# Differential attention heads: the row norm's squares folded in half, high and low part in one product with ones

## The chip, the core and the metric

The kernel runs on one core of one Trainium2 chip. The metric is device time in microseconds of one execution; the time before is the median of three runs. The engines are named as the profile names them: PE (TensorE, matrix products; PEld is its weight load), DVE (VectorE), ACT (ScalarE), POOL (GpSimd) and SP (SyncE, which only issues transfers here). SBUF is the on-chip memory of 128 partitions, PSUM the accumulator memory that PE writes.

## The reference, cut to what matters

One encoder layer of width 1024 over 512 tokens and 16 meta tokens: a stick-breaking attention branch with 8 heads, a differential attention branch with 8 heads, gates, an output projection, and a feed-forward part. All data are float32. The change is in the differential heads, in the norm of each head's output over its 128 channels:

```python
def rmsnorm(x, g):
    xf = x.astype(jnp.float32)
    y = xf * lax.rsqrt(jnp.mean(xf * xf, axis=-1, keepdims=True) + EPS)
    return (y * g.astype(jnp.float32)).astype(x.dtype)
...
    s = jnp.where(mask, s + bias[None, :, None], -jnp.inf)
    p = jax.nn.softmax(s, axis=-1)
    w = p[:, :, 0] - lam * p[:, :, 1]
    return jnp.einsum('bhqk,bhkd->bhqd', w.astype(v.dtype), v)
...
        o_df = (rmsnorm(o_df, subln_g[l]) * (1.0 - lam_init)).transpose(0, 2, 1, 3).reshape(B, L_pad, DF_V_W)
```

## The kernel before, in words

**Products in high and low parts.** Matrix operands are split into a high part (a copy rounded to fp32r, mostly by ACT) and a low part (what the rounding lost, by DVE or POOL); `split` (lines 77 to 81) issues both, at line 78 the high part and at line 81 the low one. A product of two split operands is three PE instructions, lines 296 to 298 in `mm3`: high by high, high by low, low by high.

**The differential stage.** A loop runs over 8 heads. Each head's `df_head` is a generator that yields four to six times; in between, the loop inserts pieces of other work: the next head's projections of q, k and v (`halves`, `kv_units`, `v_units`) and the partial projections of finished pairs of heads (`y_units`, whose results are copied to tiles `y_out` by ACT at line 785 and added into DRAM by transfers that POOL issues at lines 787 and 789). A head computes scores for four blocks of queries (lines 695 and 696 on PE, the biased maximum at line 699 on DVE, the exponentials at line 723 on ACT, the two maps' combination at lines 726 to 729 on DVE), turns the maps (lines 563 and 564), multiplies them with v in `weighted` (lines 296 to 298, 583, 584; the result is a PSUM tile `z`), and then norms its output.

**The norm.** The output stands with its 128 channels on the partitions and 512 tokens along the row, so that the sum over channels is a sum over partitions. It is made on PE: a product with `ones_r`, a 128x128 matrix of 1/128, gives each partition the mean. For heads 0 to 6:

- line 751: ACT copies the output from PSUM to the tile `of` (128x512);
- line 753: POOL squares it into `sq`;
- line 78: ACT casts `sq` into the high part `sqh`, and at line 81 POOL writes the low part `sql`;
- lines 758 and 759: PE multiplies `ones_r` with `sql` and with `sqh` into one PSUM tile `tr`;
- lines 760 to 765: logarithm and exponential on ACT make the reciprocal root, DVE multiplies, ACT and DVE write the normed output's parts `o_h` and `o_l`.

Lines 756 to 765 are the function `norm`, which is not run at once: it is put into the list `late` and taken out in the next head, between the scores of the second and the third block. The tiles `sqh` and `sql` use the buffers of `a_h` and `a_l`, the turned maps, which PE has read by then. Head 7 has no next head: its squares and low part are on DVE, and its norm follows one gate product later.

**What sets the order.** Only the kernel's opening has an order written by hand. In the rest a scheduler orders each engine's instructions by dependencies, by the order of the program and by its own estimate of times, and places semaphore waits. Each engine then runs its instructions strictly in that order. Weights are loaded by SP (line 210) into three buffers, split into `wh` and `wl` two or three pieces ahead of their use, and POOL issues, as background work, transfers (line 151) that prepare sums of later weights in DRAM.

Of the kernel before, what the change touches and what calls it, by code (L numbers as in the profile page):

```python
# [9 lines left out]
F32 = mybir.dt.float32  # L10
F32R = mybir.dt.float32r
BF16 = mybir.dt.bfloat16
AF = mybir.ActivationFunctionType
ALU = mybir.AluOpType
AX = mybir.AxisListType

P = 128
D = 1024
SEQ = 512
# [5 lines left out]
NH = 8  # L25
# [16 lines left out]
def block_kernel(ctx: ExitStack, tc: tile.TileContext, x, meta, norm_mix_g, w_in, w_gate, b_gate,  # L42
                 lam_q1, lam_k1, lam_q2, lam_k2, subln_g, w_br_sb, w_br_df, w_out, norm_ffn_g,
                 w_ffn_gate, w_ffn_up, w_ffn_down, norm_final_g, out):
    nc = tc.nc
# [15 lines left out]
    def tr_tile():  # L61
        return ps_mm.tile([P, 512], F32, tag="mm", name="tr")

    def z_tile():
        return ps_z.tile([P, 2, 512], F32, tag="z", name="z")
# [9 lines left out]
    cast = {}  # L75

    def split(hi, lo, src, lo_eng=None, hi_copy=None, after=None):
        cast["last"] = (hi_copy or nc.scalar.copy)(hi, src)  # L78
        if after:
            behind(cast["last"], after)  # L80
        cast["lo"] = (lo_eng or nc.vector).tensor_tensor(lo, src, hi.bitcast(F32), op=ALU.subtract)  # L81

    def behind(ins, name):
        tc.add_manual_dep(ins.ins, cast[name].ins.name,
                          mybir.DependencyInfo(mybir.DependencyClass.Sync, mybir.DependencyReason.DATA))
# [283 lines left out]
    ones_r = const.tile([P, P], F32R, name="ones_r")  # L369
# [29 lines left out]
    ap_ = att.enter_context(tc.tile_pool(name="att", bufs=1))  # L399
# [285 lines left out]
    def df_head(h, d, o_h, o_l):  # L685
        q, k = d["q"], d["k"]
        bias = ap_.tile([P, L], F32, tag="bias", name="bias")
        nc.gpsimd.tensor_scalar(bias, dist, -(2.0 ** -(h + 1)), None, op0=ALU.mult)
        mx = small.tile([P, NQ, 2], F32, tag="mx", name="mx", bufs=2)
        ls = small.tile([P, NQ, 2], F32, tag="ls", name="ls", bufs=2)  # L690
        prs = [ap_.tile([P, 2, 144 + t * P], F32, tag=f"w{t}", name="pr") for t in range(NQ)]

        def score(o, t, c, k0, k1):
            qs = slice(t * P, (t + 1) * P)
            nc.tensor.matmul(o, lhsT=q[c][:, qs], rhs=k[c][:, 0, k0:k1], start=True, stop=False)  # L695
            nc.tensor.matmul(o, lhsT=q[c][:, qs], rhs=k[c][:, 1, k0:k1], start=False, stop=True)  # L696

        def biased(t, c, zz, po, bb):
            nc.vector.tensor_tensor_reduce(po, zz, bb, scale=1.0, scalar=-3.0e38, op0=ALU.add, op1=ALU.max,  # L699
                                           accum_out=mx[:, t, c:c + 1])  # L700

        def scores(t):
            n = 144 + t * P
            z = z_tile()
            for c in range(2):
                score(z[:, c, 0:max(n, 256)], t, c, 0, max(n, 256))
            for c in range(2):
                biased(t, c, z[:, c, 0:n], prs[t][:, c], bias[:, L - n:L])
            maps(t)

        def scores3(c):
            two = lambda v: v.rearrange("p (a b) -> p a b", a=2)
            z = z_tile()
            for hf in range(2):
                score(z[:, hf, 0:HL], 3, c, hf * HL, (hf + 1) * HL)
            biased(3, c, z[:, :, 0:HL], two(prs[3][:, c]), two(bias))

        def maps(t):
            pr = prs[t]
            nm = small.tile([P, 2], F32, tag="nm", name="nm")  # L720
            nc.vector.tensor_scalar(nm, mx[:, t], -1.0, None, op0=ALU.mult)
            for c in range(2):
                nc.scalar.activation(pr[:, c], pr[:, c], AF.Exp, bias=nm[:, c:c + 1], accum_out=ls[:, t, c:c + 1])
            with tc.high_priority(offset=EVAC):
                rc = small.tile([P, 2], F32, tag="rc", name="rc")
                nc.vector.reciprocal(rc, ls[:, t])
                nc.vector.tensor_tensor(rc, rc, cn, op=ALU.mult)
                nc.vector.tensor_scalar(pr[:, 0], pr[:, 0], rc[:, 0:1], None, op0=ALU.mult)
                nc.vector.scalar_tensor_tensor(pr[:, 0], pr[:, 1], rc[:, 1:2], pr[:, 0], op0=ALU.mult, op1=ALU.add)

        scores(0)
        scores(1)
        yield 1
        if late:
            late.pop(0)()
        scores(2)
        yield 1
        scores3(0)
        yield 1
        scores3(1)  # L740
        maps(3)
        turned, av = attn_out(lambda t, k0, k1: prs[t][:, 0, k0:k1], d, 64)
        yield 3 if h < NH - 1 else 2
        turned()
        yield 2
        ps = av()
        of = ap_.tile([P, SEQ], F32, tag="of", name="of")
        sq = ap_.tile([P, SEQ], F32, tag="sq", name="sq")
        sqh = ap_.tile([P, SEQ], F32R, tag="a_h", name="sqh")
        sql = ap_.tile([P, SEQ], F32R, tag="a_l", name="sql")  # L750
        nc.scalar.copy(of, ps)
        eng = nc.gpsimd if h < NH - 1 else nc.vector
        eng.tensor_tensor(sq, of, of, op=ALU.mult)
        split(sqh, sql, sq, lo_eng=eng)

        def norm():
            pv = tr_tile()
            nc.tensor.matmul(pv, lhsT=ones_r, rhs=sql, start=True, stop=False)
            nc.tensor.matmul(pv, lhsT=ones_r, rhs=sqh, start=False, stop=True)
            nc.scalar.activation(sq, pv, AF.Ln, bias=eps_c)  # L760
            cast["norm"] = nc.scalar.activation(sq, sq, AF.Exp, scale=-0.5)
            nc.vector.scalar_tensor_tensor(sq, pv, var_max, sq, op0=ALU.is_le, op1=ALU.mult)
            nc.vector.tensor_tensor(of, of, sq, op=ALU.mult)
            nc.scalar.activation(o_h, of, AF.Copy, scale=g_sub)
            nc.vector.scalar_tensor_tensor(o_l, of, g_sub, o_h.bitcast(F32), op0=ALU.mult, op1=ALU.subtract)

        late.append(norm)


# [138 lines left out]
    def split_part(n, a, b, hi=nc.scalar.copy, lo=nc.gpsimd.tensor_tensor):  # L908
# [25 lines left out]
                            op=ALU.mult)  # L934
# [60 lines left out]
    todo = []  # L995
    for br in range(2):
        name, head = (("y_sb", sb_head), ("y_df", df_head))[br]
        if br:
            nc.gpsimd.memset(a_s, 0.0)
# [150 lines left out]
    def turned(tp_):  # L1150
        cs = slice(tp_ * 256, (tp_ + 1) * 256)
        banks = [z_tile() for _ in range(2)]
        for k in range(0, KT, 2):
            pt = banks[k // 2 % 2][:, k // 4]
            for i in range(2):
                for t in range(2):
                    nc.tensor.transpose(pt[:, (2 * i + t) * P:(2 * i + t + 1) * P],
                                        hn[:, 2 * tp_ + t, (k + i) * P:(k + i + 1) * P], ident)
            for i in range(2):
                g = g_ffn[:, k + i:k + i + 1]  # L1160
                p = pt[:, i * 256:(i + 1) * 256]
                nc.scalar.activation(hT_h[:, k + i, cs], p, AF.Copy, scale=g)  # L1162
                nc.vector.scalar_tensor_tensor(hT_l[:, k + i, cs], p, g, hT_h[:, k + i, cs].bitcast(F32),
                                               op0=ALU.mult, op1=ALU.subtract)
        for k in range(KT):
            p = banks[k // 2 % 2][:, k // 4, k % 2 * 256:(k % 2 + 1) * 256]
            if tp_ == 0:
                nc.scalar.activation(bf[k // 4][0][:, k % 4], p, AF.Copy, scale=g_ffn[:, k:k + 1])
            else:
                x, y = (bf[0][0], bf[0][1]) if k < 4 else (bf[0][1], bf[1][1])  # L1170
                cast["bf"] = nc.vector.scalar_tensor_tensor(y[:, k % 4], p, g_ffn[:, k:k + 1], x[:, k % 4], op0=ALU.mult, op1=ALU.subtract)
# [376 lines left out]
```

## Time and profile before

| | |
|---|---|
| median of 3 runs | 931.77 us (931.14 to 932.34) |
| profiled execution, its own time | 931.87 us |
| span in that profile | 930.1 us |
| instructions | 16033 |
| time of one differential head (281 to 459 us of the span) | 29.6 us |
| granted PE clock, mean | 0.999 |

In rows of the profile a line number such as L758 is a line of the kernel; an arrow reads from right to left, output from inputs; "x7" counts instructions. In rows of the timeline the first number is the start in microseconds from the start of the span, the second the duration, and a bracket tells how long the engine was idle just before and which instruction ended the wait. In the table by stretches each engine has its busy time and its number of instructions, and the last three columns are the granted PE clock (1.00 is full speed), the mean busy share of the 16 DMA engines, and what they moved. Names end without buffer numbers: `sq` of line 1441 and `sq` of line 753 are different tiles.

### The profile page before, as it was taken

Reading aid. Unit: us, or ns where it says so; the run is one execution under the profiler, and the core shown is the slowest. Engines: PE = TensorE matmul, PEld = TensorE weight load, DVE = VectorE, ACT = ScalarE, POOL = GpSimd, SP = SyncE. Lnnn points to the kernel's source line nnn. Section 1 sums busy time; section 2 is a strip of 40 time slices with the busy share of each in tenths; the row PEclk is TensorE's granted clock in tenths of the full one; section 3 lists DMA queues with packets and bytes.
Section 4 is the critical chain, followed back from the end, with each engine's and each line's share of the span. In section 5 each row is a group of like instructions: output and inputs, shape, how many; then the busy total and the mean of one; then the engine's idle time right before and its main releaser. Section 6 shows DMA issues by size and latency. Waiting matters only on the chain.

```text
span 930.1 us, 16033 instructions
## 1 busy us (share of the span) xinstructions
PE 918.8 (99%) x6010; PEld 836.9 (90%) x6010; DVE 734.3 (79%) x1413; ACT 586.1 (63%) x1104; POOL 168.4 (18%) x199
## 2 busy tenths in 40 slices
PE   8999999999999999999999999999999999999997
PEld 5999999998999899998988888899999999988886
DVE  7988877776687767976663787899888888799975
ACT  6765676676666666666665555776555555576554
POOL 3000121222333343344512000001100000000013
PEclk9999999999999999999999999999999999999999
DMA  8525598778777878799987774437744343276542
GB/s 253 139 68 168 143 212 201 169 167 250 191 192 177 217 170 182 181 211 186 197 209 181 215 260 159 127 80 183 169 118 131 91 129 98 88 274 193 192 149 91
DMA packets 155823, 158.41 MB, mean 170 GB/s; under 512 B 6465, under 2 KB 117218, under 8 KB 155746
## 3 DMA queue, kind: packets, MB, share of 16 engines
q1 hardware_dynamic: 132690, 101.61, 36.2%
q0 software_dynamic: 22896, 55.72, 29.2%
q8 instruction: 47, 0.77, 0.3%
q14 instruction: 30, 0.25, 0.1%
q10 hardware_dynamic: 160, 0.07, 0.0%
HBM read 133.64 MB, written 50.86 MB: 198 GB/s over the span
## 4 chain that ended last, share of the span: by engine, by line
PE 94%; DVE 3%; ACT 2%; issue 1%; ACTq 0%; DVEq 0%
PE mm L297 22%; PE mm L296 22%; PE mm L298 22%; PE z L297 7%; PE z L296 7%; PE z L298 7%; PE z L563 2%; PE z L696 1%; PE z L695 1%; PE tr L537 1%; DVE wl L81 1%; DVE hres L1205 1%; PE z L584 1%; PE mm L858 0%; ACT wh L78 0%
## 5 line engine op out<-in xcount | busy, mean ns | idle before, releaser
L296 PE MATMUL mm<-xT_h,wh 128*128 128x264 f32 (+2 forms) x656 | 213.6, 326 | 0.5 <-ACT xT_h L901 0.5
L297 PE MATMUL mm<-xT_l,wh 128*128 128x264 f32 (+2 forms) x656 | 213.4, 325 | 0.5
L298 PE MATMUL mm<-xT_h,wl 128*128 128x264 f32 (+2 forms) x656 | 212.5, 324 | 0.0
L78 ACT CAST wh<-wst 128x1024 fp32r<-128x1024 f32 (+1 forms) x147 | 141.5, 967 | 78.8 <-PE mm L297 56.0
L81 DVE TENSOR_TENSOR wl<-wst,wh 128x1024 fp32r<-128x1024 f32 (+1 forms) x147 | 163.1, 1114 | 31.3 <-ACT wh L78 30.9
L297 PEld LDWEIGHTS mm<-xT_l,wh 128*128 128x128 f32 x656 | 123.4, 188 | 10.3 <-DVE xT_l L902 1.3
L298 PEld LDWEIGHTS mm<-xT_h,wl 128*128 128x128 f32 x656 | 123.5, 188 | 10.0
L296 PEld LDWEIGHTS mm<-xT_h,wh 128*128 128x128 f32 x656 | 123.4, 188 | 9.9 <-ACT xT_h L901 0.9
L296 PE MATMUL mm<-hT_h,wh 128*128 128x256 f32 x304 | 84.0, 278 | 0.5 <-ACT hT_h L1162 0.5
L298 PE MATMUL mm<-hT_h,wl 128*128 128x256 f32 x304 | 84.1, 278 | 0.0
L297 PE MATMUL mm<-hT_l,wh 128*128 128x256 f32 x304 | 84.1, 277 | 0.0
L699 DVE CUSTOM_DVE_ANT_0 pr<-z,bias 128x144 f32<-128x144 f32 (+3 forms) x64 | 30.9, 501 | 34.1 <-PE z L696 31.8
L296 PEld LDWEIGHTS mm<-hT_h,wh 128*128 128x128 f32 x304 | 56.9, 188 | 0.8 <-ACT hT_h L1162 0.7
L298 PEld LDWEIGHTS mm<-hT_h,wl 128*128 128x128 f32 x304 | 57.2, 188 | 0.0
L297 PEld LDWEIGHTS mm<-hT_l,wh 128*128 128x128 f32 x304 | 57.0, 188 | 0.0
L296 PE MATMUL mm<-o_h,wh 128*128 128x512 f32 x128 | 52.4, 410 | 0.0
L297 PE MATMUL z<-wl,da 128*128 128x512 f32 (+1 forms) x132 | 50.3, 381 | 0.2 <-DVE wl L81 0.2
L296 PE MATMUL z<-wh,da 128*128 128x512 f32 (+1 forms) x132 | 50.2, 380 | 0.0
L298 PE MATMUL z<-wh,da 128*128 128x512 f32 (+1 forms) x132 | 50.2, 380 | 0.0
L298 PE MATMUL mm<-o_h,wl 128*128 128x512 f32 x128 | 50.1, 391 | 0.0
L297 PE MATMUL mm<-o_l,wh 128*128 128x512 f32 x128 | 49.9, 390 | 0.0
L151 POOL DMA_DIRECT2D ds<-in_w_ffn_down_dram x36 | 30.1, 840 | 92.0 <-ACT wh L78 62.2
(378 smaller groups left out, 2468.0 us busy)
## 6 DMA issues: line engine op xcount, KB each, us to landing
wst<-in_w_in_dram SPq DMA_DIRECT2D x40, 512.0 KB, 5.9
ds<-in_w_ffn_down_dram POOLq DMA_DIRECT2D x30, 512.0 KB, 6.2
wst<-in_w_ffn_gate_dram SPq DMA_DIRECT2D x22, 512.0 KB, 3.9
wsu<-in_w_ffn_up_dram SPq DMA_DIRECT2D x20, 512.0 KB, 3.9
wst<-in_w_gate_dram SPq DMA_DIRECT2D x16, 512.0 KB, 5.5
y_df<-y_out POOLq DMA_DIRECT2D x32, 256.0 KB, 7.2
slots<-ds SPq DMA_DIRECT2D x13, 512.0 KB, 3.2
os<-in_w_out_dram POOLq DMA_DIRECT2D x12, 512.0 KB, 5.0
```

What stands on the lines that cost most here:

```text
L78: cast["last"] = (hi_copy or nc.scalar.copy)(hi, src)
L81: cast["lo"] = (lo_eng or nc.vector).tensor_tensor(lo, src, hi.bitcast(F32), op=ALU.subtract)
L151: tc.add_manual_dep(nc.gpsimd.dma_start(dst, src, **kw).ins, cast["last"].ins.name, paced)
L296: nc.tensor.matmul(ps, lhsT=ah, rhs=bh, start=(start and i == 0), stop=False, skip_group_check=skip)
L297: nc.tensor.matmul(ps, lhsT=ah, rhs=bl, start=False, stop=False, skip_group_check=skip)
L298: nc.tensor.matmul(ps, lhsT=al, rhs=bh, start=False, stop=(stop and i == n - 1), skip_group_check=skip)
L537: nc.tensor.transpose(pt[:, j * P:(j + 1) * P], vT[:, j * P:(j + 1) * P], ident)
L563: nc.tensor.transpose(pt[:, (t - j) * P:(t - j + 1) * P], blocks(t, j * P, (j + 1) * P), ident)
L584: nc.tensor.matmul(ps.rearrange("p (t q) -> p t q", q=P)[:, :, lo_rows:P], lhsT=vf[:, 1], rhs=a_s[:, 0:4 * qn], start=False, stop=True)
L695: nc.tensor.matmul(o, lhsT=q[c][:, qs], rhs=k[c][:, 0, k0:k1], start=True, stop=False)
L696: nc.tensor.matmul(o, lhsT=q[c][:, qs], rhs=k[c][:, 1, k0:k1], start=False, stop=True)
L699: nc.vector.tensor_tensor_reduce(po, zz, bb, scale=1.0, scalar=-3.0e38, op0=ALU.add, op1=ALU.max, accum_out=mx[:, t, c:c + 1])
```

## The change

For heads 0 to 6 the squares of partitions 64 to 127 are added onto those of partitions 0 to 63 before the split, so that the sum has 64 rows; its high part goes to partitions 0 to 63 and its low part to partitions 64 to 127 of one tile, and one product with `ones_r` sums both. Head 7 keeps its way.

```diff
-        sql = ap_.tile([P, SEQ], F32R, tag="a_l", name="sql")
         nc.scalar.copy(of, ps)
-        eng = nc.gpsimd if h < NH - 1 else nc.vector
-        eng.tensor_tensor(sq, of, of, op=ALU.mult)
-        split(sqh, sql, sq, lo_eng=eng)
+        halved = h < NH - 1
+        if halved:
+            A, B = slice(0, 64), slice(64, P)
+            sq2 = ap_.tile([P, SEQ], F32, tag="a_l", name="sq2")
+            nc.gpsimd.tensor_tensor(sq[A], of[B], of[B], op=ALU.mult)
+            nc.scalar.activation(sq2[A], of[A], AF.Square)
+            nc.gpsimd.tensor_tensor(sq[A], sq[A], sq2[A], op=ALU.add)
+            cast["last"] = nc.scalar.copy(sqh[A], sq[A])
+            cast["lo"] = nc.gpsimd.tensor_tensor(sqh[B], sq[A], sqh[A].bitcast(F32), op=ALU.subtract)
+        else:
+            sql = ap_.tile([P, SEQ], F32R, tag="a_l", name="sql")
+            nc.vector.tensor_tensor(sq, of, of, op=ALU.mult)
+            split(sqh, sql, sq)
 
         def norm():
             pv = tr_tile()
-            nc.tensor.matmul(pv, lhsT=ones_r, rhs=sql, start=True, stop=False)
-            nc.tensor.matmul(pv, lhsT=ones_r, rhs=sqh, start=False, stop=True)
+            if not halved:
+                nc.tensor.matmul(pv, lhsT=ones_r, rhs=sql, start=True, stop=False)
+            nc.tensor.matmul(pv, lhsT=ones_r, rhs=sqh, start=halved, stop=True)
```

The lines after the change stand 10 further down: lines 785 and 789 are 795 and 799, the norm's products 758 and 759 are 768 and 769. In the changed program the new instructions are L755 (multiply), L756 (square on ACT), L757 (add), L758 (cast) and L759 (low part).

On POOL, the first head's norm, before and after. `y_sb` is a partial projection in DRAM to which a transfer adds a `y_out` tile, `ds` a sum of weights in DRAM; `sq_3385` is the new tile `sq2`.

```order
L753 TENSOR_TENSOR sq<-of 128x512
L81 TENSOR_TENSOR sql<-sq,sqh 128x512
L789 DMA y_sb_116<-y_out 128x512
L151 DMA ds_10_101<-in_w_ffn_down_dram 128x512
L789 DMA y_sb_117<-y_out 128x512
```

```order
L755 TENSOR_TENSOR sq<-of 64x512
L757 TENSOR_TENSOR sq<-sq,sq_3385 64x512
L799 DMA y_sb_116<-y_out 128x512
L759 TENSOR_TENSOR sqh<-sq,sqh 64x512
L151 DMA ds_10_101<-in_w_ffn_down_dram 128x512
L799 DMA y_sb_117<-y_out 128x512
```

The low part, now L759, stands behind one transfer's issue that followed it before. The same holds in all seven heads.

On ACT, at the same place: `wh` is the high part of a piece of weights, the rows of L723 are exponentials of the next head's scores.

```order
L751 COPY of<-z 128x512
L78 CAST sqh<-sq 128x512
L785 COPY y_out<-mm 128x512
L78 CAST wh<-wst 128x1024
L785 COPY y_out<-mm 128x512
L723 ACTIVATE pr,ls<-pr,nm 128x144 x2
L723 ACTIVATE pr,ls<-pr,nm 128x272 x2
```

```order
L750 COPY of<-z 128x512
L756 ACTIVATE sq_3385<-of 64x512
L795 COPY y_out<-mm 128x512
L758 CAST sqh<-sq 64x512
L78 CAST wh<-wst 128x1024
L795 COPY y_out<-mm 128x512
L723 ACTIVATE pr,ls<-pr,nm 128x144 x2
L723 ACTIVATE pr,ls<-pr,nm 128x272 x2
```

A square is added, and the first copy of a `y_out` tile now stands ahead of the cast of the squares.

On PE only the seven products L758 go; all other products keep their order. On DVE, in the next head's third block of scores, the reductions of L699 move ahead of one or two other instructions in each of the seven heads; SP's order is the same.

## Prediction

> **What bounds the kernel now.** I read the page's busy line and its chain first, then the table by stretches for the differential heads, where the change sits.
>
> ```profile
> PE 918.8 (99%) x6010; PEld 836.9 (90%) x6010; DVE 734.3 (79%) x1413; ACT 586.1 (63%) x1104; POOL 168.4 (18%) x199
> PE 94%; DVE 3%; ACT 2%; issue 1%; ACTq 0%; DVEq 0%
> core 0: us, PE busy (x) PEld busy (x) DVE busy (x) ACT busy (x) POOL busy (x), PEclk, DMA share, GB/s
> 281.00:310.56 29.56, 29.56 (x196) 27.29 (x195) 22.17 (x61) 19.64 (x45) 11.42 (x14) 1.00 0.83 202
> ...
> 428.95:458.60 29.65, 29.65 (x196) 27.30 (x195) 22.25 (x61) 19.62 (x45) 12.47 (x14) 1.00 0.96 179
> 458.60:490.00 31.40, 31.30 (x155) 26.23 (x154) 21.32 (x58) 21.22 (x42) 8.26 (x9) 1.00 0.85 204
> ```
>
> The first number behind a stretch is its length, the second PE's busy time: one head takes 29.6 us, and PE has no idle time in it at full clock. So a product that disappears there is worth the time until the next one can start, and a wait that reaches PE is paid in full. Next the waits of this stage (us in total, times, longest): PE and its weight load wait once in all, 0.5 us, in the last head, which the change leaves as it is.
>
> ```profile
> PEld tr L758 <- DVE sql L81: 0.5, 1, 0.5
> ACT wh L78 <- PE mm L297: 24.8, 20, 1.8
> SPq L210 <- DVE wl L81: 126.6, 22, 7.0
> ```
>
> **The gain: seven products.** Twelve equal products of 128x512 follow each other right behind the norm's pair; here are the first and the last of them, and the pair (start, duration).
>
> ```profile
> 286.45 0.39 PE L758 MATMUL tr<-sql,ones_r 128*128 128x512 f32 x1
> 286.68 0.39 PE L759 MATMUL tr<-sqh,ones_r 128*128 128x512 f32 x1
> ...
> 287.64 0.39 PE L296 MATMUL mm<-xT_h,wh 128*128 128x512 f32 x1
> 290.14 0.39 PE L298 MATMUL mm<-xT_h,wl 128*128 128x512 f32 x1
> ```
>
> The duration of 0.39 us overlaps the next product; what counts is the distance of starts, 2.50 us over 11 steps = 0.227 us, and the pair itself stands 0.23 apart. Heads 0 to 6 lose one each: 7 x 0.227 = 1.59 us. Bounds: nothing, and 7 x 0.39 = 2.73 if the whole duration went; I take the distance, since PE is busy from start to start. The weight load goes too, but it ran beside a product.
>
> **What is added, and whether it reaches PE.** The first norm of the seven on ACT, POOL and DVE:
>
> ```profile
> 280.19 0.59 ACT L751 COPY of<-z 128x512 f32<-128x512 f32 x1 [0.92 <-PE z L584]
> 281.94 0.62 ACT L78 CAST sqh<-sq 128x512 fp32r<-128x512 f32 x1 [1.16 <-POOL sq L753]
> 282.94 1.05 ACT L78 CAST wh<-wst 128x1024 fp32r<-128x1024 f32 x1
> 283.89 0.58 ACT L785 COPY y_out<-mm 128x512 f32<-128x512 f32 x1
> 284.53 0.42 ACT L723 ACTIVATE pr<-pr,nm 128x144 f32<-128x144 f32 x1
> 286.16 0.52 ACT L723 ACTIVATE pr<-pr,nm 128x272 f32<-128x272 f32 x1 [0.72 <-DVE nm L721]
> 290.34 1.05 ACT L78 CAST wh<-wst 128x1024 fp32r<-128x1024 f32 x1 [1.81 <-PE mm L297]
> 291.30 0.58 ACT L667 ACTIVATE dq<-mm 64x512 fp32r<-64x512 f32 x1
> ...
> 280.86 1.04 POOL L753 TENSOR_TENSOR sq<-of 128x512 f32<-128x512 f32 x1 [1.68 <-ACT of L751]
> 282.64 1.29 POOL L81 TENSOR_TENSOR sql<-sq,sqh 128x512 fp32r<-128x512 f32 x1 [0.74 <-ACT sqh L78]
> 461.45 0.86 POOL L789 DMA_DIRECT2D y_df<-y_out  x1
> 297.31 1.85 POOL L688 TENSOR_SCALAR bias<-dist 128x528 f32<-128x528 f32 x1 [4.90 <-DVE mx L699]
> 284.76 1.22 DVE L81 TENSOR_TENSOR wl<-wst,wh 128x1024 fp32r<-128x1024 f32 x1
> 303.94 0.48 PE L296 MATMUL mm<-o_h,wh 128*128 128x512 f32 x1
> ```
>
> Before, the low part ended at 282.64 + 1.29 = 283.93, 2.52 us ahead of its product at 286.45. The new chain has one step more on POOL and one on ACT, and by the order a y_out transfer is issued ahead of the low part. No row shows POOL computing on 64 partitions, or writing to other partitions than it reads. From below each such instruction could take half of its 128-partition row, from above 1.85 us, the slowest POOL row of that length; I take the rows of the same operations, because the number of elements in a partition stays 512: 1.04 with one source tile, 1.30 with two.
>
> 1. The multiply starts at 280.86 as before and ends at 281.90. Beside it ACT squares the other half, about 0.6 us by the 64x512 row, so it is done first.
> 2. The addition reads two tiles: from 281.98 (POOL handed on to POOL by a semaphore; I put 0.08, the gap from the copy at 280.78 to 280.86), 1.30, to 283.28.
> 3. ACT's cast follows 0.04 later, as 281.94 does upon 281.90, takes 0.59, and ends at 283.91. Meanwhile POOL issues the y_out transfer, 0.86: to 284.14. ACT's y_out copy now stands ahead of the cast, so that transfer waits for nothing.
> 4. The low part, two tiles: 284.14 + 1.30 = 285.44. The product's place is 286.45: 1.0 us to spare, of 2.52.
>
> So POOL's added 1.30 us, ACT's added 0.6 and the transfer are hidden under those 2.52 us; each us beyond 1.0 would cost 7. The same distance stands in the other heads (table of the tile: POOL's durations differ by 10 ns, first to last).
>
> ```profile
> L81 POOL TENSOR_TENSOR sql<-sq,sqh x7: 1295/1302/1305, 282.6 to 460.2; 128x512 fp32r<-128x512 f32 x7
> L753 POOL TENSOR_TENSOR sq<-of x7: 1041/1042/1042, 280.9 to 458.4; 128x512 f32<-128x512 f32 x7
> ```
>
> Behind ACT's cast are queued the cast of the weights at 282.94, the second y_out copy and four exponentials of the scores. They start about 0.87 us later: the weights at 283.81, ended at 284.86; the exponentials at 285.40 instead of 284.53. DVE's low part of the weights, before from 284.76 to 285.98, starts at 284.94. Those weights multiply o_h only at 303.94, 17 us later. The third exponential waits for DVE already (0.72 us idle), and ACT idles 1.81 us ahead of 290.34, so the delay ends there, at a cost of nothing; without that idle time the 0.87 us would be handed on to the rows behind, with 13 us left until PE's product at 303.94. POOL's two issues behind the low part come about 1 us later; POOL idles 4.90 us before 297.31. On DVE one or two score reductions move ahead of other work, which can only free PSUM earlier: nothing.
>
> **A lock between POOL and DVE.** Late in the kernel both read two SBUF tiles at once:
>
> ```profile
> 893.44 3.46 DVE L81 TENSOR_TENSOR wl<-slots,wh 128x1024 fp32r<-128x1024 f32 x2
> 893.60 2.22 POOL L1450 TENSOR_TENSOR outs<-hres,gF 128x512 f32<-128x512 f32 x1 [0.45 <-DVE hres L1436]
> 908.56 1.30 POOL L1451 TENSOR_TENSOR outs<-hres,gF 128x512 f32<-128x512 f32 x1 [0.44 <-DVE hres L1436]
> 908.73 2.21 DVE L81 TENSOR_TENSOR wl<-slots,wh 128x1024 fp32r<-128x1024 f32 x1
> ```
>
> Whoever starts first goes through in its own time (POOL's 1.30, at 908.56), the other waits: DVE's 1.22 becomes 2.21, POOL's 1.30 becomes 2.22. The low part used to end before DVE's work on the weights began; now it runs from 284.14 into it (284.94). POOL is first by 0.8 us, so DVE ends about 285.44 + 1.14 = 286.58 instead of 285.98 and the third exponential moves by 0.6 us, under the same idle time: nothing in the sum. The Trainium skill states this against the change (SBUF — State Buffer, section "Who interferes with whom": a DVE instruction with two SBUF inputs contends with a GpSimd instruction that reads SBUF, and issue order decides who is blocked); by that rule and by the trace, which agrees, the sum stays unless POOL comes second.
>
> **The sum.** The profiled execution took 931.87 us, 930.1 of it the span and 1.77 around it; 931.87 - 1.59 = 930.28. It lies 0.10 above the median of 931.77, so against the median 930.18. I forecast 930.2, 0.17% faster. About 0.2% (1.9 us) is what a measurement of this kernel tells from no change, so this is just short of the line, at 929.9.
>
> **Rivals** (times against the median). For the second: the y_out issue right behind the low part in two heads, the shortest and the longest of the seven at that place, and the longest anywhere of a single transfer of that line.
>
> ```profile
> 343.07 0.57 POOL L787 DMA_DIRECT2D y_df<-y_out  x1
> 431.82 0.87 POOL L789 DMA_DIRECT2D y_df<-y_out  x1
> 403.43 1.70 POOL L789 DMA_DIRECT2D y_df<-y_out  x1
> ```
>
> - *POOL's three pieces are long* (slower). If each takes 1.85 us, the multiply ends at 282.71, the addition at 284.64, the transfer's issue at 285.50, and the low part at 287.35: PE waits 0.90 us in each of seven heads, 6.3 - 1.59 = +4.7: 936.5. It decides from 4.65 us for the three together (I count 3.64). For it: shifted halves are unknown here. Against: 512 elements took 1.04 and 1.30 in every row. 8%.
> - *POOL comes second at the lock.* If the y_out issue ahead of the low part takes 1.70 us, the low part starts at 284.98, just behind DVE, takes 2.22 and ends at 287.20, 0.75 late: 7 x 0.75 - 1.59 = +3.7, 935.4. Against: at this place it took 0.57 to 0.87. 4%.
>
> - *PE's gain is given back.* The weight loads on SP wait for DVE's low parts (126.6 us in all), which now end 0.6 us later in each head, and the DMA engines are busy for 0.83 and 0.96 of the time in the two whole heads shown; if a load then comes late, or PE meets another late buffer, the 0.23 us of each head are lost: 931.8. Against: the weight casts wait for PE (24.8 us), not for a load. 14%.
>
> **How the numbers follow.** The forecast has 74%. Its own range is 929.5 to 930.9, from the spread of the three runs (931.14 to 932.34, 0.6 us either way of the median); about a third of it falls below 929.9, so faster 24%, within 50%. The given-back case adds 14% to within: 64%. The two late cases are slower: 12%. The range runs from 929.2 (the forecast, less the spread and a little of the bound of 2.73) to 932.2 (the given-back case and most of its spread); it leaves out the slower cases and a few in a hundred below.
>
> **What would show it.** Right: seven products L769 with no wait ahead of them on PE, each head some 0.23 us shorter in the table by stretches, POOL's 64x512 rows near 1.04, 1.30 and 1.30, the low part ended about 1 us before its product, DVE's weights row at that place near 1.7 us. Wrong: idle time of PE that a POOL instruction ends, POOL rows above 1.5 us, or weight casts that wait for loads.

## The result and the profile after

The changed kernel takes 937.15 us (936.19 to 937.88) against 931.45 us before (930.05 to 932.34): a ratio of 1.0057, 95% interval 1.0040 to 1.0073. Timed once more with the experiments it took 937.86 against 931.11 us, 1.0064 (1.0047 to 1.0081). The forecast was 930.2; the changed kernel is slower.

Busy time and chain of the page of the changed kernel, its table for the stretches shown of before, and what its matrix products and their weight loads wait for at line 563:

```profile
PE 918.8 (98%) x6002; PEld 835.5 (89%) x6003; DVE 740.8 (79%) x1413; ACT 591.4 (63%) x1111; POOL 176.2 (19%) x206
PE 75%; DVE 18%; ACT 3%; issue 3%; DMA 1%; DVEq 0%; ACTq 0%
281.00:310.56 29.56, 28.87 (x192) 26.55 (x191) 23.18 (x61) 20.03 (x46) 11.92 (x15) 1.00 0.80 196
428.95:458.60 29.65, 29.01 (x192) 26.57 (x191) 22.86 (x61) 20.19 (x45) 13.18 (x14) 1.00 0.92 178
PE z L563 <- DVE pr L729: 4.3, 7, 0.7
PEld z L563 <- DVE pr L729: 6.0, 7, 0.9
```

PE was busy all the time in a head; now it is idle 0.5 to 0.7 us in each (its weight load waits up to 0.9), and the wait is at line 563: the transposes of the next head's maps, the fourth of which is the first to read what DVE's last combination (line 729) writes. DVE's share of the chain goes from 3% to 18%.

The timeline of the changed kernel at the first norm, with POOL's three instructions, ACT's cast, DVE behind its score reductions, and the product:

```profile
279.50 0.59 ACT L750 COPY of<-z 128x512 f32<-128x512 f32 x1 [0.92 <-PE z L584]
280.24 1.04 POOL L755 TENSOR_TENSOR sq<-of 64x512 f32<-64x512 f32 x1 [1.75 <-ACT of L750]
281.35 1.28 POOL L757 TENSOR_TENSOR sq<-sq,sq 64x512 f32<-64x512 f32 x1
282.58 0.85 POOL L799 DMA_DIRECT2D y_sb<-y_out  x1
282.67 0.62 ACT L758 CAST sqh<-sq 64x512 fp32r<-64x512 f32 x1 [1.19 <-POOL sq L757]
282.83 0.31 DVE L699 CUSTOM_DVE_ANT_0 pr<-z,bias 128x144 f32<-128x144 f32 x1 [4.54 <-PE z L696]
283.19 1.04 ACT L78 CAST wh<-wst 128x1024 fp32r<-128x1024 f32 x1
283.50 1.29 POOL L759 TENSOR_TENSOR sqh<-sq,sqh 64x512 fp32r<-64x512 f32 x1
283.65 1.17 DVE L721 TENSOR_SCALAR nm<-mx 128x2 f32<-128x2 f32 x1
285.09 1.22 DVE L81 TENSOR_TENSOR wl<-wst,wh 128x1024 fp32r<-128x1024 f32 x1
285.77 0.40 PE L769 MATMUL tr<-sqh,ones_r 128*128 128x512 f32 x1
...
302.37 0.77 DVE L729 SCALAR_TENSOR_TENSOR pr<-pr,rc 128x528 f32<-128x528 f32 x1
303.19 0.87 PE L563 MATMUL z<-ident,pr 128*128 128x128 f32 x6 [0.69 <-DVE pr L729]
```

And DVE at the same two places before, with the weight load of the fourth transpose:

```profile
283.51 0.31 DVE L699 CUSTOM_DVE_ANT_0 pr<-z,bias 128x144 f32<-128x144 f32 x1 [4.54 <-PE z L696]
284.33 0.16 DVE L721 TENSOR_SCALAR nm<-mx 128x2 f32<-128x2 f32 x1
302.05 0.77 DVE L729 SCALAR_TENSOR_TENSOR pr<-pr,rc 128x528 f32<-128x528 f32 x1
303.14 0.14 PEld L563 LDWEIGHTS z<-ident,pr 128*128 128x128 f32 x1
```

The low part ends at 284.79 and its product starts at 285.77: it is not late. But the negation of the row maxima at line 721, an instruction on 128x2 numbers that took 0.16 us, takes 1.17 and ends when POOL's low part does. Before, POOL's low part was over at 283.93 and the negation came at 284.33. The delay does not go away again: from the first score reduction to the end of the last combination it was 302.82 - 283.51 = 19.31 us before and is 303.14 - 282.83 = 20.31 now, 1.00 more. It stands at the negation alone: from the first reduction to the start of the weights' low part (line 81) it was 284.76 - 283.51 = 1.25 us and is 285.09 - 282.83 = 2.26.

The length of the heads shows the effect without the rest of the kernel, whose time varies by 2 us and more between executions (in some of them a step of 2.3 us falls into the stick-breaking heads, ahead of the change). From the copy of the output in head 0 to that in head 6 are six heads: 457.77 - 280.19 = 177.58 us before, 460.62 - 279.50 = 181.12 after. The copies of head 6, before and after:

```profile
457.77 0.59 ACT L751 COPY of<-z 128x512 f32<-128x512 f32 x1 [0.92 <-PE z L584]
460.62 0.59 ACT L750 COPY of<-z 128x512 f32<-128x512 f32 x1 [0.92 <-PE z L584]
```

Here and below this distance is called "six heads". To head 7 it is 203.27 and 207.45, +4.18.

### The profile page after: what moved, and what is told of

Its sections match the earlier page's. It is cut to its first block, busy times and chain, and to the rows that moved or that the text cites. A ratio compares the mean times of both kernels' runs of the same rounds, so it can differ in the third digit from the quotient of the medians.

```text
span 934.7 us, 16037 instructions
## 1 busy us (share of the span) xinstructions
PE 918.8 (98%) x6002; PEld 835.5 (89%) x6003; DVE 740.8 (79%) x1413; ACT 591.4 (63%) x1111; POOL 176.2 (19%) x206
## 4 chain that ended last, share of the span: by engine, by line
PE 75%; DVE 18%; ACT 3%; issue 3%; DMA 1%; DVEq 0%; ACTq 0%
PE mm L296 17%; PE mm L297 17%; PE mm L298 17%; PE z L297 6%; PE z L296 6%; PE z L298 6%; DVE wl L81 4%; DVE pr L699 2%; PE z L563 2%; DVE pr L729 1%; DVE pr L728 1%; DMA wsu<-in_w_ffn_up_dram 1%; DVE nm L721 1%; DVE a_s L574 1%; PE tr L537 1%
## 5 line engine op out<-in xcount | busy, mean ns | idle before, releaser
L699 DVE CUSTOM_DVE_ANT_0 pr<-z,bias 128x144 f32<-128x144 f32 (+3 forms) x64 | 30.8, 500 | 33.8 <-PE z L696 31.8
L1460 POOL TENSOR_TENSOR outs<-hres,gF 128x512 f32<-128x512 f32 x4 | 6.1, 1536 | 218.1 <-issue 210.9
```

## The experiments

The theory, "held": POOL's low part, which now ends later, holds DVE's negation; DVE has no idle time from there to the turned maps, so PE waits for them. One rival, "late ACT": ACT's extra square, and the cast that waits for the addition with the weights' cast and the exponentials queued behind it, make DVE late. The other, "order": DVE's new order of the score reductions does it.

**1. The product alone taken out of the kernel before.**

```diff
-            nc.tensor.matmul(pv, lhsT=ones_r, rhs=sql, start=True, stop=False)
-            nc.tensor.matmul(pv, lhsT=ones_r, rhs=sqh, start=False, stop=True)
+            if h == NH - 1:
+                nc.tensor.matmul(pv, lhsT=ones_r, rhs=sql, start=True, stop=False)
+            nc.tensor.matmul(pv, lhsT=ones_r, rhs=sqh, start=h < NH - 1, stop=True)
```

> The kernel before with only the product taken out: in heads 0 to 6 the low part is computed as before but not multiplied with ones, so the mean is rounded. POOL and ACT keep their work; DVE gets the same new order of its score reductions as the changed kernel. 'Held' and 'late ACT': the gain of seven products, 929.5 to 930.2. 'Order': 935 to 937.

Measured: 931.87 us, ratio 1.0002 (0.9988 to 1.0016). The copies of heads 0 and 6:

```profile
282.49 0.59 ACT L751 COPY of<-z 128x512 f32<-128x512 f32 x1 [0.92 <-PE z L584]
458.73 0.59 ACT L751 COPY of<-z 128x512 f32<-128x512 f32 x1 [0.92 <-PE z L584]
```

Six heads take 176.24 us, 1.34 less: 0.223 us per product, as forecast (0.227), and no wait at line 563 in the heads. DVE's instructions stand here in the order of the changed kernel, and nothing is lost: "order" is out. In the whole time the gain did not show: the step of 2.3 us lies in this profile (its first copy stands at 282.49, not 280.19), and the spread of executions is wider than 1.6 us.

**2. The hold alone put into the kernel before.**

```diff
-        sql = ap_.tile([P, SEQ], F32R, tag="a_l", name="sql")
+        sql2 = ap_.tile([P, 2, SEQ], F32R, tag="a_l", name="sql")
+        sql = sql2[:, 0]
...
-        split(sqh, sql, sq, lo_eng=eng)
+        if h < NH - 1:
+            two = lambda v: v.unsqueeze(1).broadcast_to([P, 2, SEQ])
+            cast["last"] = nc.scalar.copy(sqh, sq)
+            cast["lo"] = eng.tensor_tensor(sql2, two(sq), two(sqh.bitcast(F32)), op=ALU.subtract)
+        else:
+            split(sqh, sql, sq, lo_eng=eng)
```

POOL writes the low part twice over in one instruction, which so takes longer; PE reads the first copy.

> The kernel before, with one edit: in heads 0 to 6 POOL's low part is computed twice in one instruction (128x1024 instead of 128x512), so that it ends about 1.1 us later, still over 1 us ahead of its product. ACT, PE and DVE have the same instructions in the same order as before. 'Held': the negation on DVE, 0.4 us behind the old end of the low part, is held 0.7 to 0.8 us, and the kernel is 2.5 to 5 us slower: 934 to 936.5. 'Late ACT' and 'order': no change, 931.5.

Measured: 933.65 us, 1.0027 (1.0016 to 1.0038). POOL, DVE and PE's wait at the maps:

```profile
282.63 2.40 POOL L758 TENSOR_TENSOR sql<-sq,sqh 128x1024 fp32r<-128x1024 f32 x1 [0.74 <-ACT sqh L757]
284.33 0.72 DVE L721 TENSOR_SCALAR nm<-mx 128x2 f32<-128x2 f32 x1
285.33 1.21 DVE L81 TENSOR_TENSOR wl<-wst,wh 128x1024 fp32r<-128x1024 f32 x1
```

```profile
PEld z L563 <- DVE pr L729: 2.0, 7, 0.3
```

The negation is held until POOL ends, although no other engine's work or order has changed, and six heads take 179.17 us, 1.59 more. So the hold by itself makes the kernel slower. The whole time grew by 2.4 us (from 931.24), just short of the 2.5 that I had put as the least; the hold was 0.56 us in this head and 0.63 or 0.64 in the others, not 0.7 to 0.8.

**3. The changed kernel with the first block's negation on ACT.**

```diff
-            nc.vector.tensor_scalar(nm, mx[:, t], -1.0, None, op0=ALU.mult)
+            if t == 0 and h > 0:
+                nc.scalar.activation(nm, mx[:, t], AF.Copy, scale=-1.0)
+            else:
+                nc.vector.tensor_scalar(nm, mx[:, t], -1.0, None, op0=ALU.mult)
```

> The changed kernel, with one edit: the negation of the row maxima of the first query block (128x2, in heads 1 to 7) runs on ACT instead of DVE. Theory 'held': POOL's low part, now later, holds DVE's negation until it is done, DVE has no idle time from there to the turned maps, and PE waits for the maps. Then the hold on the negation goes; DVE's low part of the weights behind it may still be held some 0.5 us, so 1 to 2.5 us over the kernel before (932.5 to 934), with PE's waits for the maps cut by half or more. Rival 'late ACT': the extra square and the cast that waits for the addition delay the exponentials and the weights' cast by 0.9 us, and DVE with them: about as the changed kernel, 936 to 937. Rival 'order': the score reductions that DVE now does earlier delay the maps: 936 to 937.

Measured: 933.46 us, 1.0026 (1.0014 to 1.0039). At the first norm:

```profile
286.44 1.29 POOL L762 TENSOR_TENSOR sqh<-sq,sqh 64x512 fp32r<-64x512 f32 x1
286.59 0.44 DVE L699 CUSTOM_DVE_ANT_0 pr<-z,bias 128x272 f32<-128x272 f32 x1
287.21 1.60 DVE L81 TENSOR_TENSOR wl<-wst,wh 128x1024 fp32r<-128x1024 f32 x1 [0.18 <-ACT wh L78]
```

```profile
PE z L563 <- DVE pr L732: 1.6, 7, 0.3
```

Six heads take 178.84 us: of the 3.54 us that the change added, 2.28 are gone, and PE's wait for the maps falls from 4.3 to 1.6 us. What is held now is the next instruction with two operands in SBUF, the weights' low part: 1.60 instead of 1.22. Ahead of it DVE waits another 0.18 us for ACT's high part of the weights. The reduction at line 699, which reads one operand in PSUM, passes beside POOL at 0.44. "Late ACT" alone, by which nothing was to change, is out; that it has a part is not.

**4. The changed kernel without POOL's subtraction, twice.** First the product was cut to the 64 partitions that are left:

```diff
-            cast["lo"] = nc.gpsimd.tensor_tensor(sqh[B], sq[A], sqh[A].bitcast(F32), op=ALU.subtract)
...
-            nc.tensor.matmul(pv, lhsT=ones_r, rhs=sqh, start=halved, stop=True)
+            n = 64 if halved else P
+            nc.tensor.matmul(pv, lhsT=ones_r[0:n], rhs=sqh[0:n], start=halved, stop=True)
```

> The changed kernel without the low part of the squares: POOL's last instruction of the norm is left out, and the product with ones takes the 64 partitions of the high part alone, so the mean is rounded. ACT's work and order and DVE's order stay those of the changed kernel. 'Held': POOL is done 1.3 us earlier, nothing holds DVE, the gain of seven products appears: 930 to 931.5. 'Late ACT': 936 to 937, since ACT is as late as before. 'Order': 936 to 937.

Measured: 932.88 us, 1.0016 (1.0004 to 1.0029), six heads 178.46. No wait at line 563 is left, but the heads are longer than before, which neither theory had. The reason is in the experiment itself (PE and its weight load; 64-row product, then the next one):

```profile
286.62 0.18 PEld L769 LDWEIGHTS tr<-sqh,ones_r 64*128 64x128 f32 x1 [0.35 <-ACT pr L723]
286.62 0.49 PE L769 MATMUL tr<-sqh,ones_r 64*128 64x512 f32 x1
287.04 0.19 PEld L695 LDWEIGHTS z<-dqk 128*128 128x128 f32 x1 [0.24 <-issue]
287.04 0.45 PE L695 MATMUL z<-dqk 128*128 128x400 f32 x1
```

The product before it started at 286.30. From there to the second product behind the 64-row one the starts lie 0.32, 0.42 and 0.29 us apart, instead of 0.24, 0.23 and 0.19 in experiment 1, and the same in all seven heads: 0.37 us more. Six heads are 2.22 us longer than in experiment 1, 0.37 each. The profile puts the load's wait down to ACT's line 723; in the repeat below, where the 128-row load is put down to the same line, it waits 0.04 us. So the experiment was repeated with 128 partitions, the lower half set to zero:

```diff
+            nc.gpsimd.memset(sqh[B].bitcast(F32), 0.0)
             nc.gpsimd.tensor_tensor(sq[A], of[B], of[B], op=ALU.mult)
...
-            cast["lo"] = nc.gpsimd.tensor_tensor(sqh[B], sq[A], sqh[A].bitcast(F32), op=ALU.subtract)
```

> The changed kernel without POOL's subtraction: the low half of the tile is set to zero by POOL before the multiply, so the mean is rounded; the product with ones keeps its 128 partitions, unlike in the run without a low part, whose product of 64 partitions took 0.3 to 0.5 us more of PE by itself. ACT's work is that of the changed kernel. 'Held' (two thirds of DVE's delay is POOL's hold): DVE is only some 0.3 us later than before, the differential heads (first to last copy of the output, 203.3 us before, 207.4 changed) take 201.7 to 203, about 930.5. 'Late ACT': PE waits for the maps as in the changed kernel, 206 to 207.5 us for the heads.

Measured: 930.76 us, 0.9995 (0.9983 to 1.0008). DVE behind the first score reduction, and PE's wait:

```profile
284.03 0.17 DVE L721 TENSOR_SCALAR nm<-mx 128x2 f32<-128x2 f32 x1
284.60 1.23 DVE L81 TENSOR_TENSOR wl<-wst,wh 128x1024 fp32r<-128x1024 f32 x1
```

```profile
PEld z L563 <- DVE pr L729: 0.8, 4, 0.3
```

Six heads take 177.19 us, 0.39 less than before and 3.93 less than changed, with all of ACT's added work in place. DVE's last combination ends 0.28 us later than before, counted as above. So ACT's lateness delays DVE by 0.28 us where nothing is held. This is not a share of the changed kernel's 1.00 us: there the hold alone is 1.01, and experiment 2, where ACT is not late, shows that a hold of 0.56 passes on as 0.55. In the changed kernel ACT's lateness passes beside the hold.

**5. A version without both.** ACT squares both halves from PSUM ahead of the copy, POOL's multiply goes, and the first block's negation is on ACT as in 3:

```diff
-        nc.scalar.copy(of, ps)
...
+        if not halved:
+            nc.scalar.copy(of, ps)
...
-            nc.gpsimd.tensor_tensor(sq[A], of[B], of[B], op=ALU.mult)
-            nc.scalar.activation(sq2[A], of[A], AF.Square)
+            nc.scalar.activation(sq2[A], ps[A], AF.Square)
+            nc.scalar.activation(sq[A], ps[B], AF.Square)
+            nc.scalar.copy(of, ps)
```

> A version meant to have the gain without the cost: the changed kernel, with both halves squared by ACT straight from PSUM ahead of the copy (POOL's multiply goes, its addition and subtraction come 0.7 us earlier) and the first block's negation on ACT. If hold and late ACT are the two causes, both end: DVE is no later than before, the heads take 201.7 to 202.5 us, and the time is 929.5 to 930.5. If another cause is left, 204 or more for the heads.

> The version with squares from PSUM and the negation on ACT once more: the first six heads take 176.2 us again, 1.3 us less than before and 4.9 less than the changed kernel; the time, if nothing outside the heads differs, 929.4 to 930.2.

Measured: 930.17 us, 0.9992 (0.9980 to 1.0004), and again 929.91 against 931.11 us, 0.9983 (0.9973 to 0.9992). The copies of heads 0 and 6 in the second run:

```profile
281.56 0.59 ACT L761 COPY of<-z 128x512 f32<-128x512 f32 x1
457.80 0.59 ACT L761 COPY of<-z 128x512 f32<-128x512 f32 x1
```

Six heads take 176.24 us in both runs, exactly those of experiment 1: the whole gain, no loss. In the second comparison it is faster than before, by 0.17%, and by 8 us than the changed kernel timed beside it (937.86). Counted to head 7, as in the first of these expectations, it is 200.49 us and not 201.7 to 202.5; but in heads 0 to 6 the copy now stands behind the two squares, which begin 1.23 us ahead of it (280.33 in the second run), and in head 7 it does not. Only six heads can be compared here.

With the negation left on DVE:

> The same with the negation left on DVE: POOL's low part ends about 0.7 us earlier than in the changed kernel and holds the negation 0.2 to 0.4 us. 'Held': the heads take 202 to 203.5 us, 930.5 to 931.5. If it were the number of added ACT instructions (one more than in the changed kernel), 207 us or more.

Measured: 932.72 us, 1.0015 (1.0004 to 1.0025).

```profile
283.45 1.29 POOL L761 TENSOR_TENSOR sqh<-sq,sqh 64x512 fp32r<-64x512 f32 x1
284.08 0.69 DVE L721 TENSOR_SCALAR nm<-mx 128x2 f32<-128x2 f32 x1
```

The hold is 0.53 us in this head (0.32 in two others), more than the 0.2 to 0.4 expected, and six heads take 178.13. The time is above its expectation too.

**6. Controls.** The kernel before with the same negation on ACT:

> Control: the kernel before with only the first block's negation on ACT. PE sets the pace of its heads, so nothing: 203.3 us for the heads, 931.2.

Measured: 931.57 us, 1.0005 (0.9993 to 1.0018), six heads 177.58 as before. And the changed kernel again:

> The changed kernel once more, for the size of the effect and of what varies from one execution to the next: by both theories the heads take 207.4 us again and the first six of them 181.1 (before: 177.6); the time 935 to 937.

Measured: 937.86 us (above); six heads 181.15. The lengths of heads repeat to 0.03 us, whole times do not.

All together, with DVE's delay at the end of the last combination (first head, against 19.31):

| kernel | DVE later, us | six heads, us | against before |
|---|---|---|---|
| before | 0 | 177.58 | |
| changed | 1.00 | 181.12 | +3.54 |
| 3: negation on ACT | 0.57 | 178.84 | +1.26 |
| 2: long low part, both products | 0.55 | 179.17 | +1.59 |
| 5: squares from PSUM, negation on DVE | 0.51 | 178.13 | +0.55 |
| 4: low part zero | 0.28 | 177.19 | -0.39 |
| 5: squares from PSUM, negation on ACT | 0.10 | 176.24 | -1.34 |
| 1: product less | -0.02 | 176.24 | -1.34 |

The changed kernel's heads are 0.59 us longer each at a delay of 1.00: DVE had 0.3 to 0.4 us to spare before, and what goes beyond is paid. The rows of the result agree: the weight load of the fourth transpose came 303.14 - 302.82 = 0.32 us after the last combination before, and comes 303.19 - 303.14 = 0.05 after it now. The wait itself costs more than 0.59, some 0.8 us a head, since it first eats the 0.22 us that the missing product saves.

## Why the prediction was wrong, point by point

- *The gain, 0.227 us for each product*: right, 0.223 (experiment 1).
- *POOL's chain*: right. Forecast 1.04, 1.30 and 1.30; measured 1.04, 1.28 and 1.29, on half the partitions and across them. The low part was to end 1.0 us ahead of its product and ends 0.98 ahead. The two rivals in which it would be late did not come about.
- *The lock between POOL and DVE*: the mechanism was right, its place and price were wrong. I had it stretch the weights' low part at line 81, which stands behind two reductions; it caught the negation ahead of it, which I had not listed among DVE's instructions there. The hold was 1.01 us in the first head (0.87 to 1.04 in all) instead of 0.6; the row worked from has DVE's end 1.08 us behind POOL's, not 1.14, which changes little. The row that I had read as an example showed two-operand instructions; the negation has one operand, in SBUF. The Trainium skill (SBUF — State Buffer, "Who interferes with whom") also names `tensor_scalar` among the instructions that can take both ports; the trace agrees, 1.17 against 0.16 us, even for two numbers a partition. Not every such instruction beside POOL was held: two rows of the last section show it.
- *The step that failed*: "the third exponential moves by 0.6 us, under the same idle time: nothing in the sum." The idle time was ACT's, and the row quoted for it says that DVE's line 721 ends it. The delay was DVE's, and I did not ask who waits for DVE's queue. In place of nothing, DVE's last combination came 1.00 us late, PE waited at the maps in each head, and six heads took 3.54 us more instead of 6 x 0.227 = 1.36 less. The row quoted of DVE's busy time, 22.17 of 29.56 us, hid that its idle time lies in front of the first reduction (4.54 us) and behind the turned maps; from 283.51 to 302.82 its longest gap is 0.19 us, and PE's fourth transpose followed 0.32 us behind it. PE at 100% did not mean that DVE had room.
- *ACT's queue, 0.87 us later, at no cost*: wrong by itself, since it delays DVE by 0.28 us where nothing is held (experiment 4); beside the hold no row shows it adding anything.
- *The given-back rival* let a late buffer take PE's gain. It pointed the right way, but I let the loss end at the gain (931.8), and the heads lost 3.54 us on top of it.

What stays open is a part of the whole time. Between the two profiles of the result the span grew by 4.60 us: -0.69 up to the copy of head 0, +4.18 from there to head 7, +1.10 behind it. But the two comparisons gave 5.70 and 6.75. In the repeat of the changed kernel the part behind head 7 took 450.20 us, against 446.64 before, 447.74 in the first profile of the changed kernel and 446.3 to 447.6 in the nine others. A piece of that loss is in the feed-forward part (PE busy 18.44 of 20 us, 20.00 before, 19.89 in the first profile), where DVE waits 2.7 us for two loads of weights (0.7 before, 1.4 in the first profile):

```profile
640.00:660.00 20.00, 18.44 (x158) 18.04 (x157) 16.87 (x27) 9.83 (x18) 1.76 (x2) 1.00 0.78 172
DVE s L240 <- DMA wsu<-in_w_ffn_up_dram: 2.7, 2, 2.3
```

Whether the change makes such losses more frequent was not tried.

## What to carry to other kernels

Before an instruction is moved on POOL, list everything that stands on DVE under its new place, small instructions too, and look in the traces for each kind beside that kind of POOL instruction; here a hold cost nearly all that was left of POOL's instruction even to 128x2 numbers. Then follow the delay along the queue that it falls into, to the next idle time of that same engine: an engine that is busy three quarters of the time can be full exactly where it matters. And where a gain is a fraction of the spread of whole times, compare stage lengths in the profiles: here they repeat to 0.03 us, while whole times differ by 2.

## What the runs showed of the hardware

- A DVE instruction on 128x2 numbers in SBUF was held up to 1.04 us by a POOL instruction that reads two SBUF tiles; reductions on DVE with one operand in PSUM were not (0.44 us beside POOL's low part, in experiment 3).
- Reading only SBUF does not decide it. In the kernel before, the negation of a later block ran in 0.17 us beside POOL's line 688, which reads one tile (297.31, 1.85 us), and an instruction of the same kind on 128x1 numbers ran in 0.15 us beside a POOL instruction that reads two:

```profile
298.26 0.17 DVE L721 TENSOR_SCALAR nm<-mx 128x2 f32<-128x2 f32 x1
891.75 1.40 POOL L1450 TENSOR_TENSOR outs<-hres,gF 128x512 f32<-128x512 f32 x1 [210.12 <-DVE hres L1436]
892.45 0.15 DVE L1443 TENSOR_SCALAR ssq<-ssq 128x1 f32<-128x1 f32 x1 [0.46 <-ACT sq L1441]
```

  Which property decides, no run here shows.
- A product of 64 rows between products of 128 cost PE 0.37 us more than the 128-row product in its place: the starts from the product before it on lay 0.32, 0.42 and 0.29 us apart instead of 0.24, 0.23 and 0.19, with the weight loads waiting (experiment 4).
- POOL's work on 64 partitions takes as long as on 128 (1.04 us with one source tile in both, 1.28 against 1.30 with two), also where it reads and writes different partitions.
